# A transformer layer on one core: output projection in pipelined steps, and the sums of the second half's norm spread over ten rounds

## The chip, the core and the metric

The kernel runs on one core of a Trainium2 chip. Its five engines are TensorE (PE, matrix products), VectorE (DVE), ScalarE (ACT), GpSimd (POOL) and SyncE (SP), which here issues every DMA. Each engine works through its own queue in order. The metric is the device time of one execution in microseconds (us).

## The reference, cut to what matters

One layer on x of 2048 rows (tokens) by 1024, with a modulation from a condition vector c:

```
mod = silu(c) @ w_ada + b_ada ;  sh1, sc1, g1, sh2, sc2, g2 = split(mod, 6)
h   = rms(x) * (1 + sc1) + sh1
u   = h @ w_in                    # q, k, v of 8 FoX heads and 4 differential heads
x   = x + g1 * (concat(fox(u), diff(u)) @ w_out)
h2  = rms(x) * (1 + sc2) + sh2
x   = x + g2 * ((silu(h2 @ w_gate) * (h2 @ w_up)) @ w_down)      # inner width 2816
```

rms(x) is x / sqrt(mean(x²) + eps) by row, times a gain. The change touches the first norm (h), the product with w_out and the second norm (h2). The function of attention isn't touched.

## The kernel before

The tokens are 16 row blocks of 128. Products run on float16 pairs: a value is split into a high part (a cast on ScalarE) and a low part (a subtraction on VectorE), and three products of the parts are summed. Weights are scaled by powers of two from a bound: `absmax` (L123, VectorE) takes a maximum along a row, and `colmax` (L108) sends it through a small TensorE product to take it over the partitions.

The stages in order of time, by the profiled execution: modulation, first norm and first input projections (to about 185 us), eight attention groups with the remaining input projections among them (to about 1530 us), the output projection of the 16 row blocks (about 1340 to 1603 us, at first beside the last attention group), and the MLP (to the end).

**Order.** The framework orders each engine's instructions on a timeline of its own and derives the waits. All DMAs go through SP's queue in that order, so an issue that waits for something holds back those behind it. `stage()` hands out one of three buffers of 128x1024 float32 in turn (`stg` in the profile); who takes one waits until its last user is done.

**First norm.** `first_norm(blk)` computes the row sums of squares on ScalarE, a chain of small operations for the inverse root (`rsqrt`, L126 to L136: logarithm and exponential on ScalarE and one Newton step in three VectorE operations), and scales the block on POOL. `first_hT` transposes it.

**Output projection.** `out_proj(blk)` (L917) loads the block of x into half of a buffer for a pair of blocks (`pairbuf`: `uhm` for even pairs, half of an `ht` buffer for odd ones), loads the block of the attention's result `mixed` (L924), splits it, transposes it by DMA (L928), and makes 2 × 24 matmuls (L934). L936 adds the result to x; the sum goes to DRAM (`x1d`, L937), and its inverse root mean square stays in `r2`.

**MLP.** It runs in 23 rounds q, 11 pieces of the inner width for each half of the tokens. A round has 14 slots: seven products of h2 with gate and up weights for each of w = 0 and 1 (a scheme with seven products in place of eight, so each takes one of seven sums of quarter matrices of h2, `comb(i)`), and the down product of the round before in slots of its own. `gu_load` brings 1 MB of gate and up weights into `vts`, `gu_bound` is their bound, `gu_sum` (L1038, POOL) and `gu_split` prepare them. `dn_load`, `dn_scale` and `dn_split` do this for the down weights, whose two pieces per round use stage buffers. L1125 and L1126 (POOL) end the gated product of w = 1 in `uhm`, whose bound (L123 on `uhm`) is needed for the down product.

**Second norm.** `norm_row` (L974, L975) applies it to a row block; `norm_sum` forms one of the seven sums of a pair of blocks jj: an add on POOL (L984, where the sum has two terms), the high part on ScalarE (L988), the low part on VectorE (L989), a DMA transpose. Pairs 0 to 3 (first half) are done during the output projection and land in `comb`. Pairs 4 to 7 (second half) are loaded again from `x1d` into stage buffers in rounds 2, 4, 6 and 8 (slot 8), normed in slots 9 and 10 and summed in slots 10 to 13; their transposed sums (L995) go to DRAM (`hcd`, L996) and are loaded into `comb` in round 10.

Of the kernel before, what the change touches and what calls it, by code (L numbers as in the profile page):

```python
# [9 lines left out]
F32 = mybir.dt.float32  # L10
# [45 lines left out]
def trunk(ctx, tc, t):  # L56
# [233 lines left out]
    def first_norm(blk):  # L290
        xt = xcs[blk // 4][:, blk % 4, :]
        norm_rows(xt, xt)

# [470 lines left out]
    def first_rows(c):  # L764
# [3 lines left out]
        rows = [(0, lambda: hts.append(htile()))]  # L768
        for j in range(4 * c, 4 * c + 4):
            rows.append((1, lambda j=j: first_norm(j)))  # L770
            rows.append((1, lambda j=j: first_hT(j)))
# [137 lines left out]
    hcd = dram.tile([7, 4, P, 1024], F16, tag="hcd", name="hcd")  # L909
    hs = []  # L910
# [6 lines left out]
    def out_proj(blk):  # L917
        if blk == 0:
            hs.extend(htile() for _ in range(4))
        x1 = pairbuf(blk // 2)[:, blk % 2, :]  # L920
        rows = slice(blk * P, (blk + 1) * P)
        nc.sync.dma_start(x1, t["x"][rows, :])
        mt = stage()
        nc.sync.dma_start(mt, mixed[rows, :])  # L924
# [3 lines left out]
        nc.sync.dma_start(mT.rearrange("p s k n -> p (s k) n"), mh.rearrange("p s n -> p (s n)"), transpose=True)  # L928
        for n in range(2):
# [6 lines left out]
            V.scalar_tensor_tensor(out=x, in0=b, scalar=do, in1=x, op0=ALU.mult, op1=ALU.add)  # L936
        nc.sync.dma_start(x1d[blk], x1)  # L937
# [5 lines left out]
        rsqrt(v, r2[:, blk : blk + 1], 1)  # L943

# [17 lines left out]
    def norm_load(jj, z):  # L962

        if z == 0:
            ys[jj] = {}
        ys[jj][z] = stage()
        nc.sync.dma_start(ys[jj][z], x1d[2 * jj + z])

    def norm_row(jj, z):
        if jj < 4:  # L970
            ys.setdefault(jj, {})[z] = pairbuf(jj)[:, z, :]
        y = ys[jj][z]
        blk = 2 * jj + z
        V.scalar_tensor_tensor(out=y, in0=y, scalar=r2[:, blk : blk + 1], in1=mod[:, 0:D], op0=ALU.mult, op1=ALU.mult)  # L974
        V.tensor_tensor(out=y, in0=y, in1=mod[:, D:], op=ALU.add)  # L975

    def norm_sum(jj, i):
# [12 lines left out]
        row = hl.rearrange("p k s n -> p (k s n)")  # L990
        if jj < 4:
            nc.sync.dma_start(comb(i)[:, jj], row, transpose=True)
        else:
            tr = e[:, 0:512].bitcast(F16)
            nc.sync.dma_start(tr.rearrange("p (k n) -> p k n", n=P), row, transpose=True)  # L995
            nc.sync.dma_start(hcd[ORDER.index(i), jj - 4], tr)  # L996
# [308 lines left out]
```

## Time and profile before

| | us |
|---|---|
| runs | 2925.38, 2928.06 (median), 2935.83 |
| profiled execution | 2939.51 |
| its span | 2937.7 |
| TensorE busy in the span | 2728.9 |
| VectorE busy | 2111.3 |
| ScalarE busy | 1441.2 |
| GpSimd busy | 1609.5 |

The span is from the first to the last instruction of the profiled execution. A busy engine is one that executes something, at whatever speed; for TensorE the granted clock stands beside it (1.00 is full speed). What ended an idle time is put behind an arrow in the views: "<-DVE t_amh L123" is a wait that ended when VectorE's instruction of line 123 had written its tile.

### The profile page before, as it was taken

What the parts mean: (1) busy time and instruction counts of PE and PEld (TensorE: products, weight loads), DVE (VectorE), ACT (ScalarE), POOL (GpSimd) and SP (SyncE); (2) the same over time, 40 slices, a digit from 0 to 9 for tenths busy, and PEclk for the clock granted to TensorE, in tenths of its full rate; (3) what the DMA queues carried; (4) which work ended last, traced back from release to release, by engine and by line L of the source; (5) the groups of instructions that cost most, each with busy time, mean ns of one, the idle gap of its engine ahead of it and who ended that gap; (6) DMA issues with size and microseconds to landing.
All of it is one profiled execution on the core that took longest, in us unless ns stands there. A gap on an engine that the chain in (4) does not pass through costs nothing.

```text
span 2937.7 us, 49384 instructions
## 1 busy us (share of the span) xinstructions
PE 2728.9 (93%) x18902; PEld 1479.9 (50%) x18902; DVE 2111.3 (72%) x4077; ACT 1441.2 (49%) x2725; POOL 1609.5 (55%) x1392
## 2 busy tenths in 40 slices
PE   5789989899999999999989998899999999999998
PEld 3456656566665655664444343444444444444443
DVE  7786675857758686656744887787878778778775
ACT  4666667666676777786543422333323332233230
POOL 2566666665667787675542645444545444535430
PEclk9899999999999999999999999999999999999999
DMA  6232231322224233234776223224234511112101
GB/s 230 77 82 61 63 73 39 82 53 67 73 50 94 53 105 95 49 103 118 171 196 202 85 68 98 72 79 110 70 108 150 165 59 57 58 52 64 58 22 58
DMA packets 269902, 261.92 MB, mean 89 GB/s; under 512 B 204376, under 2 KB 221144, under 8 KB 263904
## 3 DMA queue, kind: packets, MB, share of 16 engines
q1 hardware_dynamic: 269664, 258.75, 31.0%
q8 instruction: 148, 2.42, 0.4%
q14 instruction: 90, 0.74, 0.1%
HBM read 173.55 MB, written 36.91 MB: 72 GB/s over the span
## 4 chain that ended last, share of the span: by engine, by line
PE 52%; DVE 21%; DMA 12%; POOL 6%; ACT 6%; issue 4%; SPq 0%; POOLq 0%; DVEq 0%; ACTq 0%
PE ps_mx L1149 10%; PE ps_ip L437 10%; PE ps_st L1091 7%; PE ps_pv L1091 6%; DMA stg<-in_w_ada_dram 3%; PE ps_ip L934 3%; DMA stg<-stg 2%; PE ps_mx L1091 2%; PE ps_st L579 2%; DVE t_mxc L548 2%; PE ps_st L580 2%; PE ps_pv L609 2%; PE ps_mx L546 2%; PE ps_pv L608 2%; PE ps_pv L607 2%
## 5 line engine op out<-in xcount | busy, mean ns | idle before, releaser
L593 POOL TENSOR_TENSOR pxs<-pxs 128x512 f16<-128x512 f32 (+3 forms) x640 | 683.3, 1082 | 325.8 <-ACT pxs L590 191.8
L1091 PEld LDWEIGHTS <-mt 128*128 128x128 f16 x3696 | 361.8, 99 | 446.7 <-issue 22.0
L437 PE MATMUL ps_ip<-wbuf,ht 128*128 128x384 f16 (+1 forms) x2952 | 560.6, 332 | 26.1 <-DVE vts L144 13.5
L1149 PE MATMUL ps_mx<-wide,ht 128*128 128x512 f16 x2112 | 505.4, 382 | 11.5 <-ACT ht L139 5.6
L1038 POOL TENSOR_TENSOR pxm<-vts 128x512 f32<-128x512 f32 x220 | 295.7, 1370 | 347.1 <-DMA vts<-in_w_gu_dram 316.3
L585 ACT ACTIVATE pxs<-ps_st,cells 128x512 f32<-128x512 f32 (+3 forms) x640 | 388.7, 619 | 142.5 <-PE ps_st L580 68.9
L437 PEld LDWEIGHTS <-ht 128*128 128x128 f16 x3072 | 295.7, 99 | 243.5 <-issue 46.2
L1091 PE MATMUL ps_st<-ht,mt 128*128 128x512 f16 x1584 | 383.0, 386 | 5.6 <-ACT mt L1094 3.2
L1091 PE MATMUL ps_pv<-ht,mt 128*128 128x512 f16 x1584 | 383.3, 380 | 1.1 <-ACT mt L1096 1.1
L590 ACT ACTIVATE pxs<-pxs 128x512 f16<-128x512 f32 (+3 forms) x640 | 350.7, 565 | 16.4 <-PE ps_pv L609 7.6
L607 PE MATMUL ps_pv<-vts,pxs 128*128 128x129 f16 (+1 forms) x2176 | 342.6, 207 | 4.2 <-DVE os L626 3.1
L608 PE MATMUL ps_pv<-vts,pxs 128*128 128x128 f16 (+1 forms) x2176 | 344.7, 208 | 0.0
L1149 PEld LDWEIGHTS <-ht 128*128 128x128 f16 x2112 | 206.3, 98 | 266.7 <-issue 16.9
L609 PE MATMUL ps_pv<-vts,pxs 128*128 128x129 f16 (+1 forms) x2176 | 325.6, 207 | 9.8 <-POOL pxs L593 8.9
L548 DVE TENSOR_REDUCE t_mxc<-ps_mx 128x1 f32<-128x512 f32 x384 | 256.9, 682 | 93.8 <-PE ps_mx L546 92.0
L1153 DVE SCALAR_TENSOR_TENSOR mt<-ps_mx,t_ai,mt 128x512 f32<-128x512 f32 x352 | 256.6, 743 | 75.5 <-PE ps_mx L1149 75.2
L607 PEld LDWEIGHTS <-pxs 128*128 128x128 f16 x2176 | 208.2, 97 | 56.7 <-ACT pxs L585 3.5
L579 PE MATMUL ps_st<-mt 67*128 67x512 f16 (+7 forms) x640 | 223.8, 350 | 10.4 <-ACT pxs L585 10.2
L609 PEld LDWEIGHTS <-pxs 128*128 128x128 f16 x2176 | 206.8, 99 | 50.0 <-POOL pxs L593 24.3
L608 PEld LDWEIGHTS <-pxs 128*128 128x128 f16 x2176 | 208.0, 97 | 35.3 <-issue 4.1
L580 PE MATMUL ps_st<-mt 128*128 128x512 f16 (+3 forms) x640 | 223.8, 350 | 0.0
L546 PE MATMUL ps_mx<-mt 71*128 71x512 f16 (+7 forms) x640 | 197.3, 350 | 19.6 <-DVE t_mxc L548 13.1
(266 smaller groups left out, 4097.0 us busy)
## 6 DMA issues: line engine op xcount, KB each, us to landing
vts<-in_w_gu_dram SPq DMA_DIRECT2D x44, 1024.0 KB
stg<-in_w_down_dram SPq DMA_DIRECT2D x44, 512.0 KB
stg<-in_w_ada_dram SPq DMA_DIRECT2D x32, 512.0 KB
stg<-in_w_in_dram SPq DMA_DIRECT2D x24, 512.0 KB
mt<-in_w_ada_dram SPq DMA_DIRECT2D x16, 512.0 KB
mt<-mt SPq DMA_DIRECT2D x128, 64.0 KB
mixed<-os SPq DMA_DIRECT2D x32, 256.0 KB
stg<-in_w_out_dram SPq DMA_DIRECT2D x16, 512.0 KB
```

The source lines that it names most:

```text
L437: T.matmul(pt[:, 0:N], lhsT=h4[:, k, hs, c : c + P], rhs=w4[k // 4][:, k % 4, ws, 0:N], start=(i == 0), stop=(i == len(terms) - 1))
L548: V.tensor_reduce(out=mx[:, 4 * j + n : 4 * j + n + 1], in_=b[:, 0:w], op=ALU.max, axis=AX.X)
L579: T.matmul(b[:, c0:QC], lhsT=K2[0:K, kb * P : (kb + 1) * P], rhs=QA[0:K, q0:q1], start=True, stop=False, skip_group_check=True)
L585: A.activation(p32[:, c0:QC], b[:, c0:QC], AF.Exp, bias=pshift, scale=1.0)
L590: A.activation(ph[:, c0:QC], p32[:, c0:QC], AF.Copy, bias=0.0, scale=1.0)
L593: (V if hilo[1] == "V" else G).tensor_tensor(out=pl[:, c0:QC], in0=p32[:, c0:QC], in1=ph[:, c0:QC], op=ALU.subtract)
L607: T.matmul(pv[:, jj, :], lhsT=lhs_h, rhs=v4[:, kb, h, 0 : W + 1], start=first, stop=False, skip_group_check=True)
L608: T.matmul(pv[:, jj, 0:W], lhsT=lhs_h, rhs=v4[:, kb, h, W + 2 : 2 * W + 2], start=False, stop=False, skip_group_check=True)
L609: T.matmul(pv[:, jj, :], lhsT=lhs_l, rhs=v4[:, kb, h, 0 : W + 1], start=False, stop=end, skip_group_check=True)
L1038: G.tensor_tensor(out=sums[:, k * 512 : (k + 1) * 512], in0=raw[:, a * 512 : (a + 1) * 512], in1=raw[:, b * 512 : (b + 1) * 512], op=op)
L1091: T.matmul(b.rearrange("p (b n) -> p b n", b=4), lhsT=aw[w][:, APOS[i] * 4 + k, ws, :], rhs=cb[:, :, 2 * k + hb, :], start=(fresh and k == ...
L1149: T.matmul(b, lhsT=aT[:, th, as_, f, j * P : (j + 1) * P], rhs=dnb[:, (2 * q + f) % 4, ws, n * 512 : (n + 1) * 512], start=(f == 0 and z = ...
```

## The change

It has four parts.

First norm of chunks 1 to 3 (four row blocks each): the four squares are taken into one statistic of four columns, one `rsqrt` of four columns replaces four of one (`first_stats`), and the scaling follows block by block (`first_scale`).

Output projection: the load of the next block's `mixed` is issued when a block starts (`out_load`), its split and transpose after the block's first half (`out_split`). From block 9 on the second norm is applied in place to the block before (`late_row`), and the result goes to DRAM (`yd`). The preparation of the first gate and up weights is placed among the blocks 10 to 14, where it stood ahead of blocks 10 to 15.

Sums of the second half: `late_sum` gives each of the 28 sums five steps, the load of its terms from `yd` into a stage buffer, add and cast two slots later, the low part after three, transpose after four, store to `hcd` after five. Three sums start per round, in slots 6, 9 and 13 of rounds 0 to 9. The bursts of rounds 2, 4, 6 and 8 are gone.

Down weights: loads in slots 1 and 2 (3 and 4 before), bound in slots 3 and 4, split in slots 6 and 7 (9 and 10 before).

```diff
+    def first_stats(c, r4):
+        ss = small(4, "dss", bufs=2)
+        for j in range(4):
+            A.activation(sqs.bitcast(F16), xcs[c][:, j, :], AF.Square, bias=0.0, scale=1.0, accum_out=ss[:, j : j + 1])
+        V.tensor_scalar(out=ss, in0=ss, scalar1=1.0 / D, scalar2=EPS, op0=ALU.mult, op1=ALU.add)
+        r = small(4, "drr", bufs=2)
+        rsqrt(ss, r, 4)
+        r4["r"] = r
+    def first_scale(blk, r4):
+        xt = xcs[blk // 4][:, blk % 4, :]
+        G.tensor_scalar(out=xt, in0=xt, scalar1=r4["r"][:, blk % 4 : blk % 4 + 1], scalar2=0.0, op0=ALU.mult, op1=ALU.add)
...
     def out_proj(blk):
         if blk == 0:
             hs.extend(htile() for _ in range(4))
+            out_load(0)
+            out_split(0)
...
         nc.sync.dma_start(x1, t["x"][rows, :])
+        if blk + 1 < NB:
+            out_load(blk + 1)
         for n in range(2):
...
             V.scalar_tensor_tensor(out=x, in0=b, scalar=do, in1=x, op0=ALU.mult, op1=ALU.add)
+            if n == 0 and blk + 1 < NB:
+                out_split(blk + 1)
         nc.sync.dma_start(x1d[blk], x1)
...
+        if blk > 8:
+            late_row(blk - 1)
...
+    def late_row(blk):
+        y = pairbuf(blk // 2)[:, blk % 2, :]
+        norm_rows2(y, blk)
+        nc.sync.dma_start(yd[blk - 8], y)
+    def late_sum(jj, i):
...
+        def load():
+            e = st["e"] = stage()
+            for c, (z, h) in enumerate([(za, ha)] + ([other] if other else [])):
+                nc.sync.dma_start(e[:, c * 512 : (c + 1) * 512], yd[2 * jj - 8 + z][:, h * 512 : (h + 1) * 512])
...
+        def add():
+            e = st["e"]
+            if other:
+                G.tensor_tensor(out=e[:, 0:512], in0=e[:, 0:512], in1=e[:, 512:1024], op=op)
+            s3, hi, _, _ = parts()
+            A.activation(hi, s3, AF.Copy, bias=0.0, scale=1.0)
...
+        return [(0, load), (2, add), (3, low), (4, turn), (5, store)]
...
     gu_load(0, 0)
+    run(outs[10:11])
     gu_bound(0, 0)
...
+    run(outs[11:13])
     gu_scale(0, 0)
+    run(outs[13:14])
...
-    run(outs[10:16])
+    run(outs[14:16])
+    late_row(15)
...
+    late = [[] for _ in range(14 * (NQP + 1))]
+    for k, steps in enumerate([late_sum(jj, i) for jj in range(4, 8) for i in ORDER]):
+        for d, f in steps:
+            late[14 * (k // 3) + (6, 9, 13)[k % 3] + d].append(f)
...
-                at(3 + f, dn_load, q, f)
+                at(1 + f, dn_load, q, f)
+                at(3 + f, dn_bound, q, f)
             at(5, dn_scale, q)
             for f in range(2):
-                at(9 + f, dn_split, q, f)
+                at(6 + f, dn_split, q, f)
...
-        if q in (2, 4, 6, 8):
-            jj = 4 + q // 2 - 1
-            for z in range(2):
-                at(8, norm_load, jj, z)
-                at(9 + z, norm_row, jj, z)
-            for k, i in enumerate(ORDER):
-                at(min(13, 10 + k // 2), norm_sum, jj, i)
...
-            for f in st[slot]:
+            for f in late[14 * q + slot] + st[slot]:
```

On POOL, in the second part of a round with a norm, the queue of the kernel before reads as follows. L984 is the add of a norm sum, L1038 a sum of gate and up weights, L1062 the product for the down weights' bound, L1125 and L1126 the end of the gated product.

```order
L1118 TENSOR_TENSOR uhm<-mt,uhm 128x512
L1038 TENSOR_TENSOR pxm<-vts 128x512 x3
L1097 TENSOR_TENSOR mt<-mt 128x512
L984 TENSOR_TENSOR stg<-stg 128x512
L1125 TENSOR_TENSOR pxm<-pxm,wide 128x512
L1038 TENSOR_TENSOR pxm<-vts 128x512 x2
L1126 TENSOR_TENSOR uhm<-pxm,uhm 128x512
L984 TENSOR_TENSOR stg<-stg 128x512 x2
```

In the changed kernel a round of the first ten reads so (L1043 is the add of a late sum, L1100 the sum of weights, L1127 the down weights' product, L1183 as L1118, L1190 and L1191 the end of the gated product):

```order
L1187 TENSOR_TENSOR uhm<-pxm,wide 128x512
L1100 TENSOR_TENSOR pxm<-vts 128x512 x2
L1043 TENSOR_TENSOR stg<-stg 128x512
L1127 TENSOR_TENSOR stg<-stg,grep_21994 128x1024
L1043 TENSOR_TENSOR stg<-stg 128x512
L1100 TENSOR_TENSOR pxm<-vts 128x512 x3
L1183 TENSOR_TENSOR uhm<-mt,uhm 128x512
L1043 TENSOR_TENSOR stg<-stg 128x512
L1190 TENSOR_TENSOR pxm<-pxm,wide 128x512
L1191 TENSOR_TENSOR uhm<-pxm,uhm 128x512
```

Two or three adds stand in each such round, one of them still ahead of the end of the gated product, where a round with a norm had six or seven.

On SP, in one of the rounds with a norm, the queue before is this: L1060 loads down weights, L1031 gate and up weights, L967 a row block for the norm, L995 and L996 transpose and store a sum.

```order
L1060 DMA stg<-in_w_down_dram 128x1024 x2
L967 DMA stg<-x1d 128x1024
L1031 DMA vts<-in_w_gu_dram 128x2048 x2
L967 DMA stg<-x1d 128x1024
L995 DMA_TRANSPOSE stg<-stg 128x8x128
L996 DMA hcd<-stg 128x1024
```

Five more such pairs of transpose and store follow it before the next down weights. In the changed kernel a round of the first ten reads (L1122 down weights, L1093 gate and up weights, L1033 half a row block from `yd`, L1053 and L1056 transpose and store):

```order
L1122 DMA stg<-in_w_down_dram 128x1024
L1093 DMA vts<-in_w_gu_dram 128x2048
L1122 DMA stg<-in_w_down_dram 128x1024
L1033 DMA stg<-yd 128x512 x2
L1053 DMA_TRANSPOSE stg<-stg 128x8x128
L1056 DMA hcd<-stg 128x1024
L1033 DMA stg<-yd 128x512 x2
L1093 DMA vts<-in_w_gu_dram 128x2048
L1053 DMA_TRANSPOSE stg<-stg 128x8x128
L1056 DMA hcd<-stg 128x1024
L1033 DMA stg<-yd 128x512 x2
L1053 DMA_TRANSPOSE stg<-stg 128x8x128
```

The loads of weights now stand between single pairs of transpose and store, in every round and not in every second one.

At the end of the output projection SP's queue before is this (L666 stores the last attention result, L924 loads blocks 12 and up, L1179 loads x1 for the MLP's end, L928 is the transpose of a block):

```order
L1031 DMA vts<-in_w_gu_dram 128x2048
L666 DMA mixed<-os 128x4x128
L924 DMA stg<-mixed 128x1024 x3
L1174 DMA grep_22080<-grow 128x1024
L1179 DMA mt<-x1d 128x1024 x4
L924 DMA stg<-mixed 128x1024
L1031 DMA vts<-in_w_gu_dram 128x2048
L928 DMA_TRANSPOSE wide<-wide 128x16x128
```

And in the changed kernel (L1023 stores a late row to `yd`, L680, L938 and L946 are the store, the load and the transpose):

```order
L1023 DMA yd<-uhm 128x1024
L956 DMA uhm<-in_x_dram 128x1024
L1093 DMA vts<-in_w_gu_dram 128x2048
L680 DMA mixed<-os 128x4x128
L969 DMA x1d<-ht 128x1024
L938 DMA stg<-mixed 128x1024 x3
L1243 DMA grep_21994<-grow 128x1024
L946 DMA_TRANSPOSE wide<-wide 128x16x128
```

The transpose of block 12 comes before the loads of x1 and the second load of gate and up weights; stores of late rows to `yd` have come into the queue.

## Rows read from the trace of the kernel before

**Rows 1.** The page, busy time, share of the span and instructions of each engine.

```profile
PE 2728.9 (93%) x18902; PEld 1479.9 (50%) x18902; DVE 2111.3 (72%) x4077; ACT 1441.2 (49%) x2725; POOL 1609.5 (55%) x1392
```

**Rows 2.** Windows: length, busy us (instructions) by engine, granted clock, DMA share, GB/s.

```profile
1740.96:2249.73 508.77, 470.54 (x2138) 209.30 (x2136) 400.96 (x573) 155.56 (x188) 258.80 (x165) 0.97 0.31 91
2249.73:2369.93 120.20, 116.70 (x539) 52.66 (x538) 91.92 (x135) 35.79 (x41) 55.21 (x39) 0.99 0.52 173
2427.72:2542.15 114.43, 114.43 (x538) 52.07 (x536) 90.15 (x133) 35.83 (x42) 53.75 (x37) 1.00 0.17 56
```

**Rows 3.** TensorE's waits from 1640 to 2240: total us, times, longest us.

```profile
PE ps_ip L108 <- DVE t_amh L123: 28.9, 6, 7.3
PE ps_mx L1149 <- ACT ht L139: 3.6, 5, 1.1
```

**Rows 4.** Timelines of POOL, DVE and PE: start, us, instruction [idle before <-releaser].

```profile
1773.15 1.27 POOL L984 TENSOR_TENSOR stg<-stg 128x512 f32<-128x512 f32 x1 [5.08 <-DMA hcd<-stg]
...
1778.49 1.26 POOL L1126 TENSOR_TENSOR uhm<-pxm,uhm 128x512 f32<-128x512 f32 x1
...
1779.79 2.29 DVE L123 TENSOR_REDUCE t_amh<-uhm 128x1 bf16<-128x2048 f32 x1 [3.60 <-POOL uhm L1126]
...
1782.13 0.29 PE L108 MATMUL ps_ip<-idb,t_amh 128*128 128x128 bf16 x1 [7.32 <-DVE t_amh L123]
```

**Rows 5.** Line L984: POOL's idle time before it by releaser, us, times.

```profile
  DMA hcd<-stg: 101.0, 16
```

**Rows 6.** Lines L974, L975, L989 by form: min/median/max ns, first and last start.

```profile
L974 DVE SCALAR_TENSOR_TENSOR stg<-stg,cells,vts x8: 1624/1866/2281, 1684.3 to 2121.7; 128x1024 f32<-128x1024 f32 x8
L974 DVE SCALAR_TENSOR_TENSOR uhm<-uhm,cells,vts x4: 1284/1285/1286, 1369.3 to 1454.9; 128x1024 f32<-128x1024 f32 x4
...
L975 DVE TENSOR_TENSOR uhm<-uhm,vts x4: 1224/1225/1523, 1371.2 to 1456.3; 128x1024 f32<-128x1024 f32 x4
...
L989 DVE TENSOR_TENSOR stg<-stg x48: 675/835/1754, 1374.8 to 2178.9; 128x512 f16<-128x512 f32 x48
```

**Rows 7.** Windows: first norm, last attention group, end of projection, start of the MLP.

```profile
40.00:200.00 160.00, 130.55 (x869) 79.23 (x870) 116.75 (x337) 98.32 (x278) 88.91 (x86) 0.93 0.30 79
1330.00:1530.00 200.00, 183.42 (x1484) 95.00 (x1482) 131.45 (x209) 118.26 (x229) 109.91 (x94) 0.97 0.65 165
1530.00:1603.00 73.00, 64.79 (x294) 28.84 (x293) 31.65 (x51) 16.18 (x28) 20.38 (x13) 0.95 0.69 211
1603.00:1690.00 87.00, 79.50 (x354) 34.68 (x352) 70.89 (x105) 41.77 (x47) 52.80 (x33) 0.96 0.27 92
```

**Rows 8.** Timelines of PE, SP and DVE, 1529 to 1603, output projection.

```profile
1529.73 2.75 PE L934 MATMUL ps_mx<-mt,wide 128*128 128x512 f16 x12
1539.86 0.29 PE L108 MATMUL ps_ip<-idb,t_amh 128*128 128x128 bf16 x1 [7.37 <-DVE t_amh L123]
...
1560.82 3.40 PE L934 MATMUL ps_mx<-mt,wide 128*128 128x512 f16 x15
1564.06 5.34 PE L934 MATMUL ps_ip<-mt,wide 128*128 128x512 f16 x24
...
1602.88 0.38 PE L1091 MATMUL ps_st<-ht,mt 128*128 128x512 f16 x1
...
1530.65 0.95 SPq L666 DMA_DIRECT2D mixed<-os  x1
1538.30 1.28 SPq L924 DMA_DIRECT2D stg<-mixed  x3
...
1547.20 8.67 SPq L928 DMA_TRANSPOSE wide<-wide  x1
...
1542.86 2.03 DVE L144 SCALAR_TENSOR_TENSOR wide<-stg,cells,wide 128x1024 f16<-128x1024 f32 x1 [1.51 <-ACT wide L139]
```

**Rows 9.** TensorE's waits from 1330 to 1530, as in rows 3.

```profile
PE ps_ip L934 <- DMA wide<-wide: 5.7, 3, 2.3
```

**Rows 10.** Lines L133 and L230 by form, from 40 to 200, as in rows 6.

```profile
L133 DVE SCALAR_TENSOR_TENSOR t_rq<-t_ry x24: 146/159/992, 42.6 to 186.0; 128x1 f32<-128x1 f32 x15, 128x8 f32<-128x8 f32 x8, 128x4 f32<-128x4 f32 x1
...
L230 ACT ACTIVATE os<-mt x12: 1040/1057/1059, 58.6 to 137.7; 128x1024 f16<-128x1024 f32 x12
```

More of the change, by code (lines that the diff above doesn't have):

```diff
@@ L909, in trunk @@
     hcd = dram.tile([7, 4, P, 1024], F16, tag="hcd", name="hcd")
+    yd = dram.tile([8, P, D], F32, tag="yd", name="yd")
     hs = []
@@ L915, in pairbuf, with out_load, out_split @@
         return t.rearrange("p (b n) -> p b n", b=2)
[L917 to L922, printed above, removed]
+    oin = {}
+    def out_load(blk):
         mt = stage()
-        nc.sync.dma_start(mt, mixed[rows, :])
+        nc.sync.dma_start(mt, mixed[blk * P : (blk + 1) * P, :])
+        oin[blk] = mt
+    def out_split(blk):
+        mt = oin.pop(blk)
         mh, mT = scr[:, 0], scr[:, 1 + blk % 2].rearrange("p s (k n) -> p s k n", k=KT)
@@ L928, in out_proj @@
         nc.sync.dma_start(mT.rearrange("p s k n -> p (s k) n"), mh.rearrange("p s n -> p (s n)"), transpose=True)
+    def out_proj(blk):
+        if blk == 0:
+            hs.extend(htile() for _ in range(4))
+            out_load(0)
+            out_split(0)
+        mT = scr[:, 1 + blk % 2].rearrange("p s (k n) -> p s k n", k=KT)
+        x1 = pairbuf(blk // 2)[:, blk % 2, :]
+        rows = slice(blk * P, (blk + 1) * P)
+        nc.sync.dma_start(x1, t["x"][rows, :])
+        if blk + 1 < NB:
+            out_load(blk + 1)
         for n in range(2):
@@ L960, in trunk, with norm_rows2, norm_row @@
     ys = {}
[L962 to L973, printed above, removed]
+    def norm_rows2(y, blk):
         V.scalar_tensor_tensor(out=y, in0=y, scalar=r2[:, blk : blk + 1], in1=mod[:, 0:D], op0=ALU.mult, op1=ALU.mult)
         V.tensor_tensor(out=y, in0=y, in1=mod[:, D:], op=ALU.add)
+    def norm_row(jj, z):
+        ys.setdefault(jj, {})[z] = pairbuf(jj)[:, z, :]
+        norm_rows2(ys[jj][z], 2 * jj + z)
     def norm_sum(jj, i):
@@ L989, in norm_sum, with parts, low, turn @@
         V.tensor_tensor(out=hl[:, :, 1, :], in0=s3, in1=hl[:, :, 0, :], op=ALU.subtract)
[L990 to L996, printed above, removed]
+        nc.sync.dma_start(comb(i)[:, jj], hl.rearrange("p k s n -> p (k s n)"), transpose=True)
+    def late_row(blk):
[3 more added lines that the diff above has]
+    def late_sum(jj, i):
+        (za, ha), op, other = BSUM[i]
+        st = {}
+        def load():
+            e = st["e"] = stage()
+            for c, (z, h) in enumerate([(za, ha)] + ([other] if other else [])):
+                nc.sync.dma_start(e[:, c * 512 : (c + 1) * 512], yd[2 * jj - 8 + z][:, h * 512 : (h + 1) * 512])
+        def parts():
+            e = st["e"]
+            hl = e[:, 512:1024].bitcast(F16).rearrange("p (k s n) -> p k s n", k=4, s=2)
+            return e[:, 0:512].rearrange("p (k n) -> p k n", k=4), hl[:, :, 0, :], hl[:, :, 1, :], hl.rearrange("p k s n -> p (k s n)")
+        def add():
+            e = st["e"]
+            if other:
+                G.tensor_tensor(out=e[:, 0:512], in0=e[:, 0:512], in1=e[:, 512:1024], op=op)
+            s3, hi, _, _ = parts()
+            A.activation(hi, s3, AF.Copy, bias=0.0, scale=1.0)
+        def low():
+            s3, hi, lo, _ = parts()
+            V.tensor_tensor(out=lo, in0=s3, in1=hi, op=ALU.subtract)
+        def turn():
+            tr = st["e"][:, 0:512].bitcast(F16)
+            nc.sync.dma_start(tr.rearrange("p (k n) -> p k n", n=P), parts()[3], transpose=True)
+        def store():
+            nc.sync.dma_start(hcd[ORDER.index(i), jj - 4], st["e"][:, 0:512].bitcast(F16))
+        return [(0, load), (2, add), (3, low), (4, turn), (5, store)]
     def norm_pair(jj):
```

7 lines of the change are left out of this document (5 added, 2 removed).

## The prediction, made before the changed kernel was run

> **What bounds the kernel now.** I read the busy shares first, then windows of the MLP, then the waits, then the timelines around one wait. TensorE is busy 93% of the span and VectorE 72% [rows 1], so time is lost where TensorE stands still or is slow. The MLP shows both cases side by side. The last window of [rows 2] is an undisturbed pair of rounds: 114.43 us, TensorE busy in all of it, granted clock 1.00. The first window holds the four pairs of rounds with a norm of the second half: 508.77. Against 4 × 114.43 = 457.72 that is 51.05 us too much. TensorE is busy for 470.54 of it, so 38.23 us are idle and 12.82 us are matmuls at a lower clock: its mean granted clock is 0.97.
>
> The waits name the place: the column maximum of L108 waits 28.9 us in 6 waits for VectorE's bound L123 [rows 3]. The timelines show why [rows 4]. At 1773.15 a POOL sum L984 starts after 5.08 us of waiting for a store to hcd to land, because the sum's stage buffer was still in use; L1126 can't start before it on POOL's in-order queue, ends at 1779.75, VectorE's L123 starts at 1779.79, and TensorE goes on at 1782.13 after 7.32 idle. L984 waits for such stores 101.0 us in all [rows 5]. Seven sums in four slots want three buffers that the down weights also use: that is the bottleneck, and not any engine's work.
>
> **The change, part by part.** (1) Sums of the second half. The four bursts go; 28 sums come, three a round in rounds 0 to 9, each with its load two slots ahead of its add. A slot is 114.43 / 28 = 4.09 us, and five stage buffers are taken per round, so each is taken again two slots or more after its store was issued; no POOL add need wait for a store. Work per two rounds is six VectorE subtractions of 0.835 [rows 6] (5.0 us on 90.15 of 114.43), six ScalarE casts on 35.83, and at most six POOL adds on 53.75 [rows 2]; all three stay below TensorE, which covers them. Without that cover each subtraction would cost its 0.835, 23.4 us for 28. What is not in the trace is the new SP order: three transposes and three stores to hcd per round, each store waiting in SP's queue for its transpose, with the loads of gate, up and down weights behind it. Bounds: nothing, if each transpose lands within its slot, as the undisturbed pair would have it; up to the price of a stall in a norm pair, 51.05 / 4 = 12.8 us, in each round. I take 1.2 us a round, 12 us in ten: the nearest row is the small wait of L1149 for ScalarE, 3.6 us in 5 waits over the same stretch [rows 3], taken at about three such kinds. Net -51 + 12 = -39.
>
> (2) Start of the MLP. From 1603 to 1690 TensorE is busy 79.50 of 87.00 with VectorE at 70.89 [rows 7]. There the change adds two late rows (blocks 14 and 15) and the first lows: 2 × (1.285 + 1.225) + 4 × 0.835 = 8.4 us of VectorE [rows 6] against 16.1 free, but the free time lies in pieces. Bounds 0 to +8.4; I take +3. What the trace shows beside it: the same multiplication takes 1.285 us on uhm and 1.624 to 2.281 on the stage buffers, in the rounds in which POOL works [rows 6]. The Trainium skill (SBUF — State Buffer, Who interferes with whom) says that a VectorE instruction with two SBUF inputs and a GpSimd instruction that reads SBUF block each other for the whole instruction, which these rows agree with. By that rule this term would be nearer to +5 than to +3, since POOL's sums of the gate weights run there.
>
> (3) Output projection. The wait of 7.37 us at 1539.86 goes [rows 8], since the 48 matmuls of block 11 (of 108 of the projection in all, from the 12 at 1529.73 on) now stand ahead of that L108 and not behind it. At 5.34 / 24 = 0.22 us each they last from 1532.5 until about 1543. Next is block 12: its row block of the mixed output needs the last store, issued at 1530.65; its load went out at 1538.30 and its subtraction ended at 1542.86 + 2.03 = 1544.89. The changed order keeps store and load in these places behind the same 1 MB weight load, so its transpose can be issued at 1545 and not at 1547.20, with four loads of x1 less beside it. Taking 5.3 us until it lands (an estimate: what is left of the row block's way from 1547.20 to its first matmuls at 1560.82, 13.6 us, when product matmuls no longer stand between; 13.6 is the upper bound), TensorE starts block 12 at 1550.3 to 1558.6 and ends four blocks of 48 matmuls 41.5 us later, at 1591.8 to 1600. Before, the projection ended at 1602.88, with 40 product matmuls in it (8.8 us at 0.22), so at 1594.1 without them. That is -2.3 to +6. I take -2: the lower end, because fewer transfers run beside it.
>
> (4) The projection beside the last attention group. Splitting block n + 1 after the first half of block n gives its transpose a half block, 5 us, more; the waits of L934 for transposes are 5.7 us in 3 [rows 9]. I take -3, between -5.7 and +5. Late rows: each costs VectorE 1.285 + 1.225 = 2.51 us [rows 6] and SP a 512 KB store to yd. By the order two stand ahead of the last attention group's store, in a stretch with VectorE busy 131.45 of 200, and six behind it, in one with 31.65 of 73 [rows 7]: covered, so 0; uncovered the two are the +5 and the six 6 × 2.51 = +15.
>
> (5) First norm. Nine of twelve chains of small operations go (four on VectorE, one after the other, two on ScalarE); but the first scale of a chunk waits for four squares. TensorE is busy 130.55 of 160 in this stretch [rows 7], so at most 29.45 could be had. One small operation takes 0.159 us in the median [rows 10], so nine chains of four are 5.7 us of VectorE on the good side; on the bad side three chunks wait for three more squares of 1.057 us each [rows 10], 9.5 us. Bounds -5.7 to +9.5; I take -3, since the chain of a block stands on the engine that is busy 116.75 of 160 there, and the squares on one with 98.32.
>
> (6) Steps of the down weights: the earlier slots of dn_load and dn_split move work within a round in which TensorE never waits; nothing, because the undisturbed pair has 24 us free on VectorE [rows 2]; without that cover one wait per round as in (1).
>
> **Sum.** -39 + 3 - 2 - 3 - 3 = -44 us. The profiled execution took 2939.51 (span 2937.7), 11.5 above the median of 2928.06; the differences are small shares of the whole, so I take them from the median: 2884.
>
> **Rivals.** (a) The stall moves into every round. A store to hcd or a load from yd that stands in SP's queue holds back a down or gate weight load, or POOL's add stands ahead of L1126 again. Price 12.8 us per round that stalls; it breaks even at 51 / 12.8 = 4 rounds, and with the 5 us of the other terms at 4.4. With all ten: +128 - 51 - 5 = +72, 3000 us; from 6 rounds on it is slower by over 0.5%. For it: three buffers as before, and loads in two pieces of 256 KB for most sums. Against it: two slots (8.2 us) from load to add, and no seven sums in a row. Chance 0.09. (b) The gain of (1) is given back: four rounds stall, 4 × 12.8 = 51: about 2923, no change. Chance 0.13. (c) The rounds with sums don't stall but run like the pair of rounds 10 and 11, 120.20 us with granted clock 0.99 while stores and reloads go on [rows 2]: 5 × (120.20 - 114.43) = 28.9 stays of 51, so 2928 - 22 - 5 = 2901. Chance 0.16. (d) The output projection pays: the upper bound of (3) and the uncovered six rows of (4) come true, +6 + 15 in place of -5, so 2884 + 26 = 2910. Chance 0.12. (e) The forecast, with its unknowns taken together, 2865 to 2897: chance 0.50.
>
> **How the numbers follow.** The forecast is 2884. Half a per cent is 14.6 us, about what a measurement of this kernel can tell from no change: faster means below 2913.4, slower above 2942.7. Faster: all of (e) and (c), (d) but for a part, a part of (b): 0.50 + 0.16 + 0.10 + 0.02 = 0.78. Same: 0.02 + 0.10 + 0.01 = 0.13. Slower: 0.08 of (a) and 0.01 of (b): 0.09. The range of 8 in 10 runs from 2856, where the residual of (1) is nothing and every other term is at its better end (-51 - 2.3 - 5.7 - 5.7 = -64.7, so 2863, and the 7 us below it are the distance of the median run to the slowest one), to 2922, which leaves out (a) and most of (b).
>
> **What would show it.** Right: no wait of POOL for hcd stores, no L108 wait over 2 us for L123 in rounds 1 to 9, two-round windows of 115 to 119 at a clock of 0.99 or 1.00; the wait ahead of the first L108 in the projection gone and one for block 12's transpose there. Wrong: two-round windows of over 122 in rounds 0 to 9, or VectorE as releaser of over 25 us of TensorE's waits from 1340 to 1700, or waits for weight loads in the MLP.

## The result and the profile after

The changed kernel took 2952.46 us in the median of four runs (2949.82 to 2954.51), against 2929.69 of four runs of the kernel before: a ratio of 1.0077 with a 95% interval of 1.0058 to 1.0096. The forecast was 2884, with 2856 to 2922 as range. The change made the kernel slower.

The page and windows of the changed kernel follow: busy time of the engines, then four pairs of rounds from round 2 on (marked by the same instruction as before, a ScalarE copy in the second half of a round), each of these pairs by itself, and an undisturbed pair. The columns of the windows are those of [rows 2].

```profile
PE 2733.7 (93%) x18902; PEld 1482.7 (50%) x18902; DVE 2123.6 (72%) x4041; ACT 1434.5 (49%) x2704; POOL 1603.2 (54%) x1392
...
1751.28:2260.91 509.63, 470.23 (x2140) 208.50 (x2139) 378.17 (x553) 152.65 (x180) 242.87 (x162) 0.98 0.30 94
...
1751.28:1880.01 128.73, 116.39 (x536) 51.48 (x535) 97.34 (x141) 39.14 (x48) 63.22 (x43) 1.00 0.31 98
1880.01:2005.99 125.98, 116.01 (x526) 51.29 (x524) 93.15 (x139) 38.31 (x46) 56.87 (x40) 0.97 0.32 98
2005.99:2139.55 133.56, 121.47 (x540) 53.17 (x539) 94.18 (x139) 38.83 (x47) 62.49 (x41) 0.96 0.30 91
2139.55:2260.91 121.36, 116.35 (x543) 52.55 (x542) 93.50 (x137) 36.37 (x41) 60.29 (x41) 1.00 0.26 87
...
2437.11:2551.47 114.36, 114.36 (x537) 52.12 (x536) 89.94 (x133) 35.73 (x41) 53.61 (x37) 1.00 0.16 56
```

The eight rounds that took 508.77 us with the bursts [rows 2] take 509.63 with the spread sums: 39.40 us idle where 38.23 were, and in both 12.8 us more of busy TensorE than four undisturbed pairs have. Nothing of the 51 us came back.

Ten rounds, from that copy in round 0 to the one in round 10, took 619.2 us before and 628.0 after. They began 2.4 us later (1632.91 and not 1630.55), and from round 12 on the two kernels run alike: together that is about the difference of the two spans, 2947.9 and 2937.7. The medians lie 22.8 us apart, because the profile of the kernel before is of one of its slower executions and that of the changed kernel of its fastest; for the other 12.6 us there is no profile.

The long waits are gone and many short ones came. TensorE's longest waits of the changed kernel in the ten rounds, then those of VectorE, SP and POOL at the sums (total us, times, longest us):

```profile
PE ps_ip L108 <- DVE t_amh L123: 17.5, 8, 5.0
PE ps_mx L1214 <- DVE mt L1218: 9.6, 8, 1.7
PE ps_st L1156 <- DVE pxm L1164: 5.6, 5, 1.9
...
DVE stg L1049 <- ACT stg L1045: 72.0, 19, 7.9
DVE t_amh L123 <- POOL uhm L1191: 21.4, 9, 7.8
...
SPq L1056 <- DMA stg<-stg: 50.8, 25, 4.5
...
SPq L1033 <- DMA hcd<-stg: 34.6, 17, 5.0
...
POOL stg L1043 <- DMA stg<-yd: 48.4, 9, 9.3
```

POOL no longer waits for stores to hcd [rows 5]; the SP queue does (L1033 is the load of a sum's terms), POOL waits for the load (L1043 is the add), and VectorE stands 72 us ahead of the low parts (L1049, after the cast L1045) and 21.4 us ahead of the bound of the gated product, which POOL's L1191 ends, at times behind such an add. All the waits of TensorE above end with VectorE, and none in the ten rounds is for a load of weights. One sum of round 4 shows the chain, by the timelines of SP, POOL, ACT, DVE and PE (start, us, instruction, idle time before it and what ended it):

```profile
1874.73 0.33 SPq L1122 DMA_DIRECT2D stg<-in_w_down_dram  x1
1875.93 0.33 SPq L1033 DMA_DIRECT2D stg<-yd  x1
1881.88 1.24 SPq L1053 DMA_TRANSPOSE stg<-stg  x1
1884.98 0.33 SPq L1056 DMA_DIRECT2D hcd<-stg  x1
1887.01 0.79 SPq L1033 DMA_DIRECT2D stg<-yd  x2
...
1908.35 0.33 SPq L1056 DMA_DIRECT2D hcd<-stg  x1
1910.36 0.33 SPq L1122 DMA_DIRECT2D stg<-in_w_down_dram  x1
...
1890.62 1.27 POOL L1043 TENSOR_TENSOR stg<-stg 128x512 f32<-128x512 f32 x1 [6.55 <-DMA stg<-yd]
...
1891.92 0.63 ACT L1045 ACTIVATE stg<-stg 128x512 f16<-128x512 f32 x1 [11.34 <-POOL stg L1043]
...
1892.59 0.69 DVE L1049 TENSOR_TENSOR stg<-stg 128x512 f16<-128x512 f32 x1 [4.70 <-ACT stg L1045]
1893.62 1.28 DVE L144 SCALAR_TENSOR_TENSOR mt<-vts,t_ws,mt 128x1024 f16<-128x1024 f32 x1 [0.35 <-ACT mt L139]
1894.83 0.74 DVE L1218 SCALAR_TENSOR_TENSOR mt<-ps_mx,t_ai,mt 128x512 f32<-128x512 f32 x1
...
1895.62 1.46 PE L1214 MATMUL ps_mx<-wide,ht 128*128 128x512 f16 x6 [1.67 <-DVE mt L1218]
...
1933.07 3.06 DVE L144 SCALAR_TENSOR_TENSOR wide<-stg,t_dws,wide 128x1024 f16<-128x1024 f32 x2 [0.97 <-ACT wide L139]
```

The sum before stores at 1884.98; the next load goes out at 1887.01, when that store has landed; add, cast and low part follow 3.6, 4.9 and 5.6 us after the load. Two slots would be 8.2 us. VectorE had reached the low part 4.70 us too early, and its evacuation of a down product (L1218), for which TensorE waits, stands behind it.

Why does the load wait for the store of the sum before, with three buffers? The loads of the down weights take theirs early. In the undisturbed rounds both go out right behind the last split, and their own split comes 56 us later, in a round of 57.2 (timelines of DVE and SP):

```profile
2485.32 3.06 DVE L144 SCALAR_TENSOR_TENSOR wide<-stg,t_dws,wide 128x1024 f16<-128x1024 f32 x2 [0.96 <-ACT wide L139]
...
2487.21 1.52 SPq L1122 DMA_DIRECT2D stg<-in_w_down_dram  x2
...
2543.69 4.21 DVE L144 SCALAR_TENSOR_TENSOR wide<-stg,t_dws,wide 128x1024 f16<-128x1024 f32 x2
```

In the rounds with sums the load at 1874.73 does the same: it goes ahead of the round's first sum, and the three sums of the round and the next down weights (1910.36) pass one buffer, one after the other. From then until the split at 1933.07 three pieces of down weights (loaded at 1851.03, 1874.73 and 1910.36) hold all three buffers, so the three sums are pressed into some 36 us of a round of 63.

### The profile page after: what moved, and what is told of

Its sections match the earlier page's. It is cut to its first block, busy times and chain, and to the rows that moved or that the text cites. A ratio compares the mean times of both kernels' runs of the same rounds, so it can differ in the third digit from the quotient of the medians.

```text
span 2947.9 us, 49485 instructions
## 1 busy us (share of the span) xinstructions
PE 2733.7 (93%) x18902; PEld 1482.7 (50%) x18902; DVE 2123.6 (72%) x4041; ACT 1434.5 (49%) x2704; POOL 1603.2 (54%) x1392
## 4 chain that ended last, share of the span: by engine, by line
PE 49%; DVE 20%; DMA 15%; POOL 6%; ACT 5%; issue 4%; SPq 1%; POOLq 0%; DVEq 0%; ACTq 0%
PE ps_ip L451 10%; PE ps_mx L1214 9%; PE ps_st L1156 6%; PE ps_pv L1156 6%; DMA stg<-in_w_ada_dram 3%; DMA stg<-stg 2%; DMA vts<-in_w_gu_dram 2%; DVE t_mxc L562 2%; PE ps_st L593 2%; PE ps_mx L1156 2%; PE ps_st L594 2%; DMA stg<-yd 2%; PE ps_ip L964 2%; PE ps_mx L560 2%; PE ps_pv L623 2%
## 5 line engine op out<-in xcount | busy, mean ns | idle before, releaser
L1214 PE MATMUL ps_mx<-wide,ht 128*128 128x512 f16 x2112 | 506.9, 382 | 18.4 <-DVE mt L1218 9.6
L1100 POOL TENSOR_TENSOR pxm<-vts 128x512 f32<-128x512 f32 x220 | 288.1, 1335 | 355.1 <-DMA vts<-in_w_gu_dram 330.6
L1218 DVE SCALAR_TENSOR_TENSOR mt<-ps_mx,t_ai,mt 128x512 f32<-128x512 f32 x352 | 257.2, 744 | 66.4 <-PE ps_mx L1214 65.8
L560 PE MATMUL ps_mx<-mt 71*128 71x512 f16 (+7 forms) x640 | 197.9, 351 | 17.5 <-DVE t_mxc L562 13.0
```

What stands on the lines that cost most here:

```text
L1100: G.tensor_tensor(out=sums[:, k * 512 : (k + 1) * 512], in0=raw[:, a * 512 : (a + 1) * 512], in1=raw[:, b * 512 : (b + 1) * 512], op=op)
L1214: T.matmul(b, lhsT=aT[:, th, as_, f, j * P : (j + 1) * P], rhs=dnb[:, (2 * q + f) % 4, ws, n * 512 : (n + 1) * 512], start=(f == 0 and z = ...
```

## The experiments

Each ran beside the kernel before on the same chip; a ratio is to that kernel, with its 95% interval. "Ten rounds" is the stretch just named, from the profile of each kernel; "low parts" is VectorE's idle time ahead of the 28 low parts. The medians of the kernel before that stand behind the ratios lie between 2927.92 and 2933.79. The rounds of e4 and e7 are those of the kernel before, and their ten rounds differ from its 619.2 by up to 4.5 us, so smaller differences in that column tell nothing.

| kernel | us | ratio | ten rounds, us | low parts, us |
|---|---|---|---|---|
| before | 2929.69 | 1 | 619.2 | |
| after | 2952.46 | 1.0077 (1.0058 to 1.0096) | 628.0 | 72.0 |
| e1 own buffers | 2922.78 | 0.9956 (0.9937 to 0.9975) | 597.7 | 29.6 |
| e2 no sums | 2879.29 | 0.9814 (0.9799 to 0.9829) | 566.9 | |
| e3 late sums alone | 2950.88 | 1.0057 (1.0042 to 1.0072) | 625.6 | 72.9 |
| e4 projection alone | 2933.92 | 1.0003 (0.9990 to 1.0016) | 620.1 | |
| e5 paced, own buffers | 2891.84 | 0.9877 (0.9862 to 0.9892) | 577.2 | 17.0 |
| e6 paced, stage buffers | 2892.58 | 0.9881 (0.9863 to 0.9899) | 579.3 | 17.3 |
| e7 first norm alone | 2925.99 | 0.9996 (0.9981 to 1.0011) | 614.7 | |
| e8 down slots alone | 2927.77 | 0.9996 (0.9984 to 1.0009) | 615.6 | |
| e9 paced, no lag | 2895.98 | 0.9898 (0.9875 to 0.9921) | 579.8 | 18.8 |
| e10 paced down weights | 2933.23 | 1.0017 (1.0003 to 1.0031) | 597.0 | 5.9 |
| e11 late rows alone | 2926.91 | 0.9997 (0.9983 to 1.0012) | 608.5 | |
| e12 paced sums alone | 2894.32 | 0.9891 (0.9870 to 0.9911) | 575.4 | 18.4 |
| e13 paced, one own buffer | 2904.30 | 0.9913 (0.9889 to 0.9936) | 584.4 | 37.7 |
| e14 one own buffer | 2931.01 | 1.0000 (0.9987 to 1.0014) | 615.2 | 53.3 |

### Which part loses: the four parts one by one

**Late sums alone** (the kernel before with `late_row`, `yd` and `late_sum`, bursts out).

```diff
+    late = [[] for _ in range(14 * (NQP + 1))]
...
-        if q in (2, 4, 6, 8):
...
-            for f in st[slot]:
+            for f in late[14 * q + slot] + st[slot]:
```

> The kernel before with one part of the change alone: late rows in the output projection and the late sums three per round; first norm, projection steps and slots of the down weights as before. Theory 1: the rounds are as in the changed kernel (no gain over the bursts) and the late rows cost up to 8 us in the projection: 2928 to 2945. If the loss of the change sits in the projection's steps or in the slots of the down weights, this kernel shows the gain that was forecast for the sums: 2885 to 2905.

Ratio 1.0057, 625.6 us in the ten rounds. Theory 1 has the kind right, but the loss is larger than it allowed (2950.88, and 2945 was its upper end). This part alone has most of the loss.

**Projection alone.**

```diff
+            if n == 0 and blk + 1 < NB:
+                out_split(blk + 1)
...
+    run(outs[10:11])
     gu_bound(0, 0)
```

> The kernel before with the output projection's steps alone (load and split of the next block ahead, first gate and up weights prepared among the blocks), without late rows; the norm of the second half in bursts as before. If the late rows and their stores to yd, which held back the last store of the mixed output in SP's queue by 4.3 us, are the cause of the 7.8 us lost by the start of the MLP: 2922 to 2930, with the wait for block 12's transpose at 4 to 7 us. If the placement of the bound among the blocks is the cause (VectorE stands 7 us at it, block 12's split behind it): 2930 to 2938, with that wait near 10 us again.

No change (1.0003), as the second theory had it, but the wait is as the first had it. Its wait for block 12's transpose is 4.4 us, in the changed kernel 10.7 (TensorE's waits from 1500 to 1612, and from 1520 to 1615):

```profile
PE ps_ip L948 <- DMA wide<-wide: 4.4, 1, 4.4
```

```profile
PE ps_ip L964 <- DMA wide<-wide: 10.7, 1, 10.7
```

SP's timeline of e4, then of the changed kernel:

```profile
1535.00 0.38 SPq L666 DMA_DIRECT2D mixed<-os  x1
...
1540.15 1.27 SPq L922 DMA_DIRECT2D stg<-mixed  x3
```

```profile
1534.91 0.38 SPq L680 DMA_DIRECT2D mixed<-os  x1
...
1542.38 1.27 SPq L938 DMA_DIRECT2D stg<-mixed  x3
```

The store of the mixed output is not issued later in the changed kernel, as I had written. But the loads behind it, which wait until it has landed, go out 2.2 us later there, and VectorE did a late row's first half (L997, 1.27 us) just ahead of the split of block 12. Together that is the 3.4 us by which the transpose left later (1551.04 and not 1547.63). Why the store took longer to land wasn't tried; the load of x that waits for a store to yd went out beside it, at 1534.02 and not at 1529.13.

**First norm alone, slots of the down weights alone.**

```diff
-            rows.append((1, lambda j=j: first_norm(j)))
+            rows.append((0.5, lambda j=j: first_scale(j, r4)))
```

```diff
-                at(3 + f, dn_load, q, f)
+                at(1 + f, dn_load, q, f)
+                at(3 + f, dn_bound, q, f)
```

> The kernel before with the batched first norm alone. My prediction gave -3 us (-5.7 to +9.5); the changed kernel's first attention groups run 4 to 6 us earlier than before, up to about 830 us, and the lead is gone by 1110. If that loss of the lead is chance or contention there: 2924 to 2931. If the lead holds: 2924 to 2926, with the end of attention 4 to 6 us earlier.

> The kernel before with the earlier slots of the down weights alone. In the trace the two loads go out right behind the last split and the weights hold two of three stage buffers for nearly a whole round, whatever the slots say. If the slots don't matter: 2927 to 2934. If an earlier split frees the buffers for the bursts: 2910 to 2925.

Both 0.9996 with intervals across 1. The slots of the down weights don't matter, as the early loads say. For the first norm the interval is wider than the 3 us in question.

**Late rows alone**, with bursts that load the normed rows.

```diff
-        nc.sync.dma_start(ys[jj][z], x1d[2 * jj + z])
+        nc.sync.dma_start(ys[jj][z], yd[2 * jj + z - 8])
```

> The kernel before with the eight late rows and their stores to yd alone; the bursts of rounds 2, 4, 6 and 8 load the normed rows from yd and leave their own two norm rows out. Late rows cost 3 to 8 us by the start of the MLP if the stores in SP's queue are what delays the projection there; the bursts give back 0 to 8 us (two rows of 3.3 us less on VectorE each, four times, where VectorE is not the bound). Together 2925 to 2938. If late rows are the larger part of the loss of 17 us of the sums alone: 2940 to 2950.

0.9997: no loss, with 608.5 us in the ten rounds, 10.7 less than before (6 to 7 less than e7 and e8). The late rows are paid for. The loss is the sums'.

### What in the sums loses

**No sums.**

```diff
-    for k, steps in enumerate([late_sum(jj, i) for jj in range(4, 8) for i in ORDER]):
+    for k, steps in enumerate([]):
...
-                if q == NPAIR - 1 and w == 1:
+                if False:
```

> The changed kernel without the 28 late sums (load, add, cast, low part, transpose, store) and without the reload of the second half's sums in round 10; late rows and everything else stay. It gives the price of the sums in the rounds. Theory 1 and theory 2 both put the loss of rounds 0 to 9 on the sums: two rounds at 114.5 to 116, in all 45 to 60 us less than 2952, so 2892 to 2907. A third theory (the rounds are slow for another reason, as the earlier steps of the down weights, or the clock after the output projection): more than 2915.

This kernel leaves out the 28 sums and their reload in round 10, so the second half of the tokens gets no new sums; it serves to price them. 2879.29, some 73 us below the changed kernel, more than expected. The ten rounds take 566.9; the 28 sums cost 61.1 us there, 2.2 us each.

**Buffers of their own** (two, in the half of `vts` that is free after the last late row).

```diff
-            e = st["e"] = stage()
+            e = st["e"] = own[(7 * (jj - 4) + ORDER.index(i)) % 2]
```

> The changed kernel, but the late sums of the MLP use two buffers of their own (the half of vts that is free after the last late row) and not the three stage buffers. Theory 1 (the sums pass one stage buffer in series, since the down weights hold the other two: each load waits for the store of the sum before, and VectorE's queue stands at the low part, 64.6 us in 16 waits): VectorE's wait for the cast falls below 25 us, two rounds take 116 to 120 us and the total falls by 20 to 40 us from 2952, to 2912 to 2932. Theory 2 (the sums' work itself, on VectorE and POOL beside each other, or SP's queue with three transposes per round): less than 10 us change, 2945 to 2955.

2922.78, as theory 1 had it; the low parts, at 29.6, are a little above its 25. But the rounds were not 58 to 60 each: the 28 sums were done by 1841 us, in about four rounds of up to 72 us, and from round 5 on the rounds took 57. With more buffers the order ran the sums as fast as the buffers allowed.

**Pacing.** So the next two tied each load to the product of its slot, by a copy of one column of that product into the buffer ahead of the load, with own buffers and with stage buffers.

```diff
+            A.activation(e[:, 0:1], now["b"][:, 0:1], AF.Copy, bias=0.0, scale=1.0)
+            A.activation(e[:, 512:513], now["b"][:, 0:1], AF.Copy, bias=0.0, scale=1.0)
             for c, (z, h) in enumerate([(za, ha)] + ([other] if other else [])):
...
                 product(q, w, i)
+                now["b"] = sets[q]["b", w, {2: 4, 3: 5}.get(i, i)]
```

> As the kernel with own buffers for the late sums, but each load also waits for the product of its slot (ScalarE copies one column of that product into the buffer before the load), so that three sums go per round as the change means it and not seven in each of the first rounds. Theory 1 (only the shared stage buffer spoils the lag): rounds 1 to 9 at 57.2 to 58.5 us each, total 2890 to 2910. Theory 2 (each sum costs TensorE 1.5 to 2 us wherever it runs, by the work on VectorE and POOL or by SP's queue; seven per round cost 14 us a round with own buffers): 60 to 63 us per round, total 2920 to 2935 as with own buffers alone.

> The changed kernel with the same extra copies of one column ahead of each load, sums still in the stage buffers. It shows what the pacing alone does. Theory 1: nothing, since the stage buffer already paces the sums: 2945 to 2960, rounds of 62 to 66 us, low parts still waiting 50 us or more in all. If pacing is what helps: 2900 to 2920.

2891.84 and 2892.58. The first was expected by theory 1, the second was not: I had taken the stage buffer as the pace. The tie does more than pace. In the order that comes of it the loads of the down weights no longer go ahead of the round's sums, so that two sums have a buffer each; the SP timeline of e6 shows four loads and no store between them, and the down weights (L1124) behind the stores. Its loads of sums (L1035) waited for a store once in the ten rounds, where those of the changed kernel did 17 times, and TensorE's waits at L108 fell from 17.5 to 0.5 us (last two lines):

```profile
1858.15 4.38 SPq L1035 DMA_DIRECT2D stg<-yd  x4
1865.76 1.24 SPq L1055 DMA_TRANSPOSE stg<-stg  x1
1868.82 0.33 SPq L1058 DMA_DIRECT2D hcd<-stg  x1
1869.24 1.30 SPq L1055 DMA_TRANSPOSE stg<-stg  x1
1872.29 0.33 SPq L1058 DMA_DIRECT2D hcd<-stg  x1
1873.26 0.33 SPq L1095 DMA_DIRECT2D vts<-in_w_gu_dram  x1
1873.65 0.42 SPq L1124 DMA_DIRECT2D stg<-in_w_down_dram  x1
...
SPq L1035 <- DMA hcd<-stg: 1.7, 1, 1.7
...
PE ps_ip L108 <- DVE t_amh L123: 0.5, 1, 0.5
```

**No lag.** The paced kernel with all five steps in the slot of the load.

```diff
-        return [(0, load), (2, add), (3, low), (4, turn), (5, store)]
+        return [(0, load), (0, add), (0, low), (0, turn), (0, store)]
```

> As the paced kernel with stage buffers (2892.6), but all five steps of a late sum stand in the slot of its load: no lag of two slots between load and add in the program. Theory A (the spread over the round and over two buffers is what helps, the lag written into the program does not decide): 2885 to 2900, low parts waiting 15 to 30 us in all. Theory B (the lag is what keeps VectorE's queue from standing): the low parts wait 50 us or more again, 2920 to 2950.

2895.98, low parts 18.8: theory A. The two slots of lag in the program decide nothing once the loads are tied; without the tie this wasn't tried.

**Paced down weights.** The tie at the loads of the down weights, the sums as in the change.

```diff
         e["st", f] = stage()
+        A.activation(e["st", f][:, 0:1], now["b"][:, 0:1], AF.Copy, bias=0.0, scale=1.0)
```

> The changed kernel with the down weights' loads, and not the sums', tied to the product of their slots (1 and 2), so that they can't go out right behind the last split and take the second buffer before the sums of the round. Theory 1 again (the down weights hold two of three buffers, the sums of a round pass the third in series): the sums get two buffers, low parts wait below 35 us, 2890 to 2920. Theory C (the sums must be tied to their slots themselves, otherwise the order puts them back to back into VectorE's queue): 2935 to 2955.

2933.23, between the two theories' ranges. VectorE's wait at the low parts went from 72.0 to 5.9 us, and that of a sum's load for a store from 34.6 to 16.7, so the early loads of the down weights do put the sums in series; but the ten rounds fell by 31.0 us, not by 50. Some of what is missing is the tie's own price: the eight rounds from the copy in round 13 to that in round 21, which have no sums, took 7.9 us more than in e6. Where the rest comes from stays open.

**One buffer.** Sums in one buffer of their own, with and without the tie, each with all steps in the load's slot. The cut is against e5 and e1.

```diff
-            e = st["e"] = own[(7 * (jj - 4) + ORDER.index(i)) % 2]
+            e = st["e"] = own[0]
```

> All late sums pass one buffer of their own (half of the free half of vts), each load tied to the product of its slot, all steps written in the load's slot. Theory S (the series through one buffer is the cause): the loads of a round still wait for the store before, the low parts wait 50 us or more in all, 2920 to 2950. Theory B (back to back is the cause: a sum whose steps stand in the engines' queues right behind the one before makes VectorE's queue stand for its load; apart, one buffer is enough): low parts 15 to 35 us, 2885 to 2905.

> The same single buffer of their own, loads not tied to a slot, so that the sums follow each other as fast as the buffer lets them; the down weights have all three stage buffers. Theory S and theory B: the low parts wait 50 us or more, the rounds in which the sums run take 63 us or more, total 2920 to 2950. If the sharing with the down weights (their loads waiting for a sum's store) is what costs: 2885 to 2905.

2904.30 with the tie and 2931.01 without. The second leaves the stage buffers to the down weights and is no better than the kernel before, so the sharing alone isn't what costs. With e1 and e5 they make a square (those two have the lag in the program, which e9 found without effect in a tied kernel):

| ten rounds (low parts), us | not tied | tied |
|---|---|---|
| one own buffer | 615.2 (53.3) | 584.4 (37.7) |
| two own buffers | 597.7 (29.6) | 577.2 (17.0) |

Theory S falls: in series through one buffer, but tied, the sums cost 17.5 us over e2 and not 50. Theory B has the times right; its 15 to 35 us at the low parts was a little low, and the second buffer takes 21 to 24 us of that wait away by itself. The tie is worth 31 us with one buffer and 20 with two.

**Paced sums alone** on the kernel before, in stage buffers.

> The kernel before with late rows and late sums alone, each load tied to the product of its slot; first norm, projection and slots of the down weights as before. If the pacing is all that the change lacked: 40 to 60 us less than the same kernel without it (2950.9), so 2890 to 2910, equal to the paced change within 8 us, since the other three parts measured within 0.1% of no change. If the slots of the down weights are needed for it: 2915 to 2935.

2894.32, within 3 us of the paced change: with the tie the sums alone bring 1.1%, and the other three parts add nothing that can be measured. TensorE is busy in nearly all of the eight rounds that cost 508.77 us [rows 2] before:

```profile
1738.70:2204.40 465.70, 461.49 (x2154) 209.25 (x2153) 387.17 (x553) 159.02 (x226) 243.82 (x163) 1.00 0.34 108
```

e5, e6, e9 and e12 are 1.0 to 1.2% faster than the kernel before. The tied change (e6) gains 36 us where 44 were forecast for the change.

## Why the prediction was wrong

**Step (1), the sums: wrong, and the step that failed has a name.** I wrote that "five stage buffers are taken per round, so each is taken again two slots or more after its store was issued; no POOL add need wait for a store". I counted buffers by the slots of the program. The order has no slots: a load goes out when its buffer is free. The trace of before had the fact that breaks the count, in its undisturbed rounds: there too the down weights are loaded right behind the last split and hold two buffers for nearly a whole round. In the bursts of [rows 4] and [rows 5], on which I rested, they don't. There the two row blocks of the norm hold two buffers until the last sum has read them, the seven sums pass the third in series, and the down weights come behind (SP and POOL before):

```profile
1679.53 0.33 SPq L967 DMA_DIRECT2D stg<-x1d  x1
...
1735.58 0.33 SPq L967 DMA_DIRECT2D stg<-x1d  x1
...
1792.77 0.81 SPq L1060 DMA_DIRECT2D stg<-in_w_down_dram  x2
...
1791.48 1.26 POOL L984 TENSOR_TENSOR stg<-stg 128x512 f32<-128x512 f32 x1 [8.74 <-DMA hcd<-stg]
```

The change took the row blocks out of the stage buffers, and the down weights came into their place. So loads went on waiting for stores, on SP and not on POOL, and the residue that I set at 1.2 us a round measured 61.1 / 10 = 6.1. Term (1) was to be -39; the ten rounds measured +8.8. What the bursts cost (51 us) was right, and so was the chain from POOL's wait for a store to TensorE; who held the buffers was not. e12 gets 43.8 us of the ten rounds back.

**Rival (a)** came true: every round stalls. No wait of TensorE is for a load of weights, but POOL's add does stand ahead of the gated product's end again (L1191, L1126 before). In round 6 it waits for its load, L1191 and the bound follow it, and TensorE waits (POOL, DVE and PE):

```profile
2035.79 1.26 POOL L1043 TENSOR_TENSOR stg<-stg 128x512 f32<-128x512 f32 x1 [3.56 <-DMA stg<-yd]
...
2039.99 2.29 DVE L123 TENSOR_REDUCE t_amh<-uhm 128x1 bf16<-128x2048 f32 x1 [0.50 <-POOL uhm L1191]
...
2042.33 0.29 PE L108 MATMUL ps_ip<-idb,t_amh 128*128 128x128 bf16 x1 [3.06 <-DVE t_amh L123]
```

VectorE's low parts, where it stands longest, were not among the rival's paths. Three of the four pairs of rounds are over the 122 us that I gave as a sign of being wrong. Its price of 12.8 us was too high, since waits of mostly 1 to 3 us took the place of one of 6 to 7. I gave it 0.09 for two reasons. Two slots from load to add is the same miscount; no seven sums in a row is true, but three in a row through one buffer were enough. Its own point for, "three buffers as before", deserved to be followed to the holders of the other two.

**Step (2), start of the MLP:** +3 forecast; from the first copy of round 0 (in its first half) to the fourth copy it was 78.4 us before and 75.9 after. That shows no loss, but the first copy of the changed kernel stands in ScalarE's queue behind a sum's cast that had waited 3.2 us for its load, so a few us could hide there. The rule on VectorE and GpSimd (the Trainium skill, SBUF — State Buffer, Who interferes with whom) would have made it dearer, and the times don't show that; single low parts do spread as it says, 675 to 2177 ns, and the five longest (2157 to 2177) each began while GpSimd worked on L1127.

**Steps (3) and (4), projection:** -5 together forecast. The wait moved to block 12's transpose as written, at 10.7 us where the estimate gave 7.3, and the 24 matmuls behind it took 8.17 us in place of 5.34, at a granted clock of 0.64, which the sum had left out. The projection ended at 1601.2 with 9 product matmuls in it; reckoned as in the prediction that is 1599.2 against 1594.1, the upper end of its range. (From 1529.73 on the projection has 252 matmuls and not the 108 that I wrote; no term uses that number.) In (4), from 1330 to 1530, the 5.7 us of waits for transposes went, but TensorE's waits for VectorE's L966 rose from 5.8 (L936 before) to 10.4. But in kernels whose medians stand within 0.05% of the kernel before, the first copy of the MLP came anywhere from 1593.5 (e8) to 1606.3 us (e4), so a few us of one profile are no finding. By the medians, the projection alone and the late rows alone are within 0.2% of nothing.

**Steps (5) and (6):** first norm -3 forecast, 0.9996 measured; down slots nothing, 0.9996 measured. Right, as far as they can be told from zero.

**Sum.** The sums alone give +0.57%, the change +0.77%. The difference is smaller than the width of either interval, so it may be nothing.

## What to carry to other kernels

A slot in the program is not a time on the chip: where a scheduler orders the queues, ask for each buffer who holds it from which load to which last use, in the trace, before counting on a lag. Work that is spread to hide its waits has to be tied to where it is wanted; if only a free buffer starts it, it starts at once, and the in-order queues of the engines that finish it stand. Idle time of VectorE ahead of a step "off the path" is the row to watch: over the kernels with sums the ten rounds follow it roughly, from 575 us at 18 to 628 at 72, though e10 shows that it isn't all.

## What was not expected of the hardware

Short waits cost the clock in some rounds and not in others. In the pair of rounds from 1751.28 to 1880.01 TensorE stood still for 12.3 of 128.73 us, in waits of which the longest is 2.0 us, and the granted clock of the window is 1.00. In the next pair the longest wait is 1.9 us, and the granted clock is 0.97. Two of its waits stand close together, and the clock fell to half of full speed in the second (PE, then windows of the changed kernel):

```profile
1978.88 0.23 PE L108 MATMUL ps_ip<-idb,t_amh 128*128 128x128 bf16 x1 [1.83 <-DVE t_amh L123]
...
1981.67 5.28 PE L1156 MATMUL ps_st<-ht,mt 128*128 128x512 f16 x12 [1.91 <-DVE pxm L1164]
...
1966.00:1980.30 14.30, 11.32 (x52) 4.84 (x51) 4.84 (x3) 1.71 (x3) 11.49 (x9) 1.00 0.26 74
1980.30:1987.20 6.90, 5.53 (x14) 1.98 (x14) 5.48 (x13) 2.35 (x3) 2.36 (x1) 0.51 0.07 30
```

The third and the fourth pair, with waits of up to 3.1 and 2.2 us, have 0.96 and 1.00. The bursts' rounds, with single waits of up to 7.3 us [rows 3], had 0.97 [rows 2]. The longest single wait of a stretch doesn't tell its clock here.
